# A hybrid mixer block with a gated FFN: staging places, four weight pieces and one product moved around the change of halves

## The chip, the core and the metric

The kernel runs on one core of a Trainium2 chip. The metric is the device time of one execution in microseconds (us), as the median of several runs; less is better. The core has a matrix engine (PE, with its weight loads shown as PEld), a vector engine (DVE), a scalar engine (ACT), a general engine (POOL), and SP, which here does nothing but issue the DMA transfers. Each engine works through its own queue in order, and the queue's order is fixed before the kernel runs.

## The reference

2048 tokens of width 1024 pass one residual block of three mixers with gates, then an FFN with a short convolution, then a norm. The part that the change touches is the second line, the last line, and the end of the first.

```
x = x + merged @ w_o                      # merged: three gated mixers of rms_norm(x)
x = x + conv_ffn(rms_norm(x, norm_ffn_g), ...)
return rms_norm(x, norm_final_g)

def conv_ffn(h, w_in, conv_w, conv_b, w_out):
    u, gv = split(h @ w_in, 2)            # 2816 columns each
    uc = conv_w[0]*u[t-2] + conv_w[1]*u[t-1] + conv_w[2]*u[t] + conv_b
    return (gelu(uc) * gv) @ w_out
```

## The kernel before

Every float32 matrix product is done as three matmuls on operands split into a rounded high part and the remainder. The tokens go through the mixers in four tiles of 512 (the loop at L1031), which write x after the mixers, channels on the partitions, to a buffer x2d in device memory.

The FFN then works on two halves of 1024 tokens. A half has 22 blocks f of 128 FFN columns. in_block (L827) does a block's two input products (u and gv, for two token tiles) with seven block products in place of eight, in the order 1, 2, 6, 5, 3, 7, 4. Each of the seven is twelve matmuls (L837 to L839) of a weight piece against an operand list B[m], and goes into one of four PSUM banks named mm. DVE combines them into u (L868 to L877) and the gate (L880, L881, L883); the convolution is L847 to L849, gelu L850, and gated (L860) writes the result G, split in two, by L861 to L863. At every second block the function mid runs out_group (L913) between product 2 and product 6: it multiplies the G of the two blocks before with w_ffn_out, in 16 tiles of six matmuls (L899 to L901) on banks named ch and mx, and DVE adds each tile to the accumulator acc in SBUF (L903).

Weight pieces live in a ring (ring_tile, L112): six tiles (three wsp, SV, UV, BK), or four while RING[:-2] is set (blocks 2 to 4 of the second half, and the last two blocks of a half). In the first half in_piece (L804) builds a block's seven pieces from four raw weight tiles, 11, 12, 21 and 22 of keepf (L693), with DVE sums at L818 to L821 and a split by ACT and POOL (L823, L824), and stores each to a cache. In the second half it loads the piece from the cache in one transfer of 512 KB. w_out (L886) loads a raw output piece into one of three tiles wraw and splits it (L136, L137).

The operands B of a half are made by ffn_prep (L701), a generator of eight steps. A step loads quarters (128 channels x 512 tokens) of x2d, multiplies each by the norm's factors on DVE (L710), forms differences (minus, L718, DVE) and splits them with ACT and POOL (put, L713 to L715). Steps 1 to 4 load two quarters each, all into wraw; steps 5 to 8 load four each: b11 into the keepf tile 11, b12 into wraw, b22 into 22, b21 into wraw. For the first half, step by step, they go between the products with w_up_rwkv and w_o of the last mixer tile; for the second half, between the tiles of the last two output groups (step, L907). The normalising rows themselves lie in the tiles s1 and 12.

The final norm of the first half is done while the second half begins: after its block 0, finish_sum (L749) squares and sums acc into tiles taken from the ring; after block 1, finish_rstd (L761) and finish_scale (L769) scale acc (ACT, POOL L782, DVE L784) and store it to out, 16 transfers, and load_acc (L962) loads the second half's start values from x2d into the same tiles, 16 more. All DMA is issued by SP from L88, in one queue.

The order of each engine's queue is set by the framework's planner, which takes instructions by priority (the order of the program, raised inside high_priority) as they become ready by its own estimate; the order in the trace therefore differs from the program's at places.

Of the kernel before, what the change touches and what calls it, by code (L numbers as in the profile page):

```python
# [10 lines left out]
F32 = mybir.dt.float32  # L11
# [3 lines left out]
ALU = mybir.AluOpType  # L15
# [4 lines left out]
P = 128  # L20
D = 1024
KB = D // P
TT = 512
# [39 lines left out]
RING = [("wsp", WB)] * WB + [("SV", 1), ("UV", 1), ("BK", 1)]  # L63
# [3 lines left out]
SEVEN = {1: "11", 2: "12", 6: "11", 5: "s1", 3: "12", 7: "21", 4: "22"}  # L67
# [14 lines left out]
def block_kernel(ctx: ExitStack, tc, A, out, T=2048):  # L82
    nc = tc.nc
    NT = T // TT
    te, ve, sc, gp = nc.tensor, nc.vector, nc.scalar, nc.gpsimd
# [18 lines left out]
    sb = ctx.enter_context(tc.tile_pool(name="sb", bufs=1))  # L104
# [17 lines left out]
    ring = {"n": 0, "tags": RING}  # L122

    def ring_tile(dt=F32R):
        tag, bufs = ring["tags"][ring["n"] % len(ring["tags"])]
        ring["n"] += 1
        return sb.tile([P, 2, 512], dt, tag=tag, name="wsp", bufs=bufs)
# [572 lines left out]

    def ffn_prep(hf, B):  # L701

        rsb = [keepf["s1"], keepf["12"]]
        for t in range(2):
            bcast(rsb[t], rs2d[hf * 1024 + t * TT:hf * 1024 + t * TT + TT])

        def quarter(k, t, place=None):
            b = sb.tile([P, 512], F32, tag="wraw", name="wraw", bufs=3) if place is None else keepf[place]
            dma(b, x2d[k, :, hf * 1024 + t * TT:hf * 1024 + t * TT + TT])
            ve.scalar_tensor_tensor(b, b, cc("norm_ffn_g", k), rsb[t], ALU.mult, ALU.mult)  # L710
            return b

        def put(o, src):  # L713
            sc.copy(o[:, 0], src)
            gp.tensor_tensor(o[:, 1], src, o[:, 0].bitcast(F32), ALU.subtract)  # L715

        def minus(dst, a, b):
            ve.tensor_tensor(dst, a, b, ALU.subtract)  # L718

        def blocks(t):  # L720
            return [t[:, :, k, :] for k in range(4)]

        hA = sb.tile([P, 2, 2, 4, TT], F32R, tag="hA", name="hA")
        B[1], B[2] = blocks(hA[:, 0]), blocks(hA[:, 1])
        for k in range(4):
            put(B[1][k], quarter(k, 0))
            put(B[2][k], quarter(4 + k, 0))
            yield
        for m, tag in ((6, "g16"), (5, "z16"), (3, "macc"), (7, "ya")):
            B[m] = blocks(sb.tile([P, 2, 4, TT], F32R, tag=tag, name=f"B{m}"))  # L730
        B[4] = [sb.tile([P, 2, TT], F32R, tag=t, name="B4", bufs=2) for t in ("LP", "LP", "BKt", "BKt")]
        for k in range(4):
            b11, b12, b22, b21 = quarter(k, 0, "11"), quarter(k, 1), quarter(4 + k, 1, "22"), quarter(4 + k, 0)
            minus(b11, b12, b11)
            put(B[5][k], b11)
            minus(b12, b22, b12)
            put(B[3][k], b22)
            minus(b11, b22, b11)
            put(B[6][k], b11)
            put(B[7][k], b12)  # L740
            minus(b21, b11, b21)
            put(B[4][k], b21)
            yield
# [25 lines left out]
    def finish_scale(hf, acc, tk, ssums, o, rs):  # L769
        n = tk.stop - tk.start  # L770
        on_pool = range(1, KB, 2) if n == TT else (1, 3, 5) if tk.stop < 1024 else (1, 3, 5)
        for d in on_pool:
            ac = acc_view(acc, d, tk)
            sc.activation(ac, ac, AF.Identity, scale=cc("norm_final_g", d))
        rp = rows_of(rs, n // P)[:, :n]
        rb = (ring_tile(F32)[:, 0] if o is None else sb.tile([P, TT], F32, tag="LP", name="rb", bufs=2))[:, :n]
        sc.copy(rb, rp)
        for d in range(KB):
            ac = acc_view(acc, d, tk)
            dst = ac if o is None else o[:, d]  # L780
            if d in on_pool:
                gp.tensor_tensor(dst, ac, rb, ALU.mult)  # L782
            else:
                ve.scalar_tensor_tensor(dst, ac, cc("norm_final_g", d), rp if len(ssums) > 2 else rb, ALU.mult, ALU.mult)  # L784
            cols = slice(hf * 1024 + tk.start, hf * 1024 + tk.stop)
            if o is None:
                dma(out[d, :, cols], ac)
            elif d % 2:
                dma(out[d - 1:d + 1, :, cols].rearrange("k p t -> p k t"), o[:, d - 1:d + 1])

    def ffn(prep):
# [8 lines left out]
        acc_tags = [("rq", 1), ("rta", 1), ("rsq", 1), ("rrn", 1), ("rkk", 1), ("rQ", 1), ("rys", 1), ("ry2", 1),  # L800
                    ("bonus", 2), ("bonus", 2), ("sgd", 1), ("rrs", 1), ("rks", 1), ("rvs", 2), ("rvs", 2)]
        B = prep
        for hf in range(T // 1024):
            def in_piece(f, n, m):  # L804

                w = ring_tile()
                hi, lo = w[:, 0], w[:, 1]
                if hf > 0:
                    dma(w.bitcast(F32), cache[7 * f + n])
                    return w  # L810
                if n == 0:
                    for r in ("11", "12", "21", "22"):
                        k0 = 512 * (r[1] == "2")
                        dma(keepf[r], A["w_ffn_in"][f + NF * (r[0] == "2"), :, k0:k0 + 512])
                K = keepf
                with tc.high_priority():
                    if n == 2:
                        ve.tensor_tensor(K["s1"], K["21"], K["22"], ALU.add)  # L818
                        ve.tensor_tensor(K["21"], K["11"], K["21"], ALU.subtract)
                        ve.tensor_tensor(K["11"], K["s1"], K["11"], ALU.subtract)  # L820
                        ve.tensor_tensor(K["12"], K["12"], K["11"], ALU.subtract)  # L821
                    src = K[SEVEN[m]]
                    sc.copy(hi, src)  # L823
                    gp.tensor_tensor(lo, src, hi.bitcast(F32), ALU.subtract)  # L824
                return w

            def in_block(f, G, mid):  # L827
# [40 lines left out]
                ve.tensor_tensor(U0[:, 2:TT + 2], product(2), s1, ALU.add)  # L868
                carry(U0)
                uc0 = conv(U0)  # L870
                if mid is not None:
                    mid()
                ve.tensor_tensor(s1, s1, product(6), ALU.add)
                m5 = product(5)
                U1 = u_tile()
                ve.tensor_tensor(U1[:, 2:TT + 2], m5, s1, ALU.add)
# [102 lines left out]
            for f in range(NF):  # L979
# [17 lines left out]
                if hf > 0 and f == 0:  # L997
                    old_su = []
                    for t in range(2):
                        su = ring_tile(F32)  # L1000
                        old_su.append([su[:, k] for k in range(2)])
                        finish_sum(hf - 1, old, slice(t * TT, t * TT + TT), old_su[t])
                if f == 1:
                    if hf == 0:
                        x2_stats(NT - 1)
                    else:
                        for t in range(2):
                            tk = slice(t * TT, t * TT + TT)
                            rs = finish_rstd(tk, old_su[t])
                            finish_scale(hf - 1, old, tk, old_su[t], None, rs)  # L1010
                    load_acc()
# [282 lines left out]
```

## Time and profile before

| | |
|---|---|
| median of three runs | 3422.11 us (3419.94 to 3427.18) |
| profiled execution | 3428.93 us, span 3427.1 us |
| PE busy | 3172.2 us (93% of the span) |
| DVE busy | 2146.0 us (63%) |
| ACT, POOL busy | 1122.3 us (33%), 986.3 us (29%) |
| DMA | 573.83 MB, mean 167 GB/s |

Times in the rows count from the start of the span. A busy time is that of instructions running, and an idle time is put down to the instruction or transfer whose end came last before the engine went on. Matmuls overlap, so that a matmul's own length (0.39 us) is more than the distance between two of them.

### The profile page before, as it was taken

How to read it: one execution, taken by the hardware profiler on the slowest of the kernel's cores; microseconds unless marked ns; L12 is line 12 of the kernel's file. 1: busy time of each engine (PE TensorE's matmuls, PEld its weight loads, DVE VectorE, ACT ScalarE, POOL GpSimd, SP SyncE). 2: the span in 40 equal slices, each digit the busy share in tenths (PEclk: the TensorE clock that was granted, in tenths of full speed). 3: DMA queues.
4: the chain of work that ended last, by engine and by line, in shares of the span. 5: the costliest groups of instructions: out<-in, count | busy, mean ns of one | idle time of the engine just before them, and what ended most of it. 6: DMA issues, size and time to landing. Idle time of an engine off the chain costs nothing. (4 is left out here: it accounts for less than half of the span.)

```text
span 3427.1 us, 44883 instructions
## 1 busy us (share of the span) xinstructions
PE 3172.2 (93%) x16224; PEld 2489.8 (73%) x16224; DVE 2146.0 (63%) x3950; ACT 1122.3 (33%) x2055; POOL 986.3 (29%) x1128
## 2 busy tenths in 40 slices
PE   6988898999999999999999899999999879999998
PEld 4656676767777677776767677777777668888887
DVE  3987641877436876437874666667667745555556
ACT  3545342433223352223333333233233312121223
POOL 3444443122111221011221644344345511010103
PEclk9999999999999999999999999999999889999999
DMA  7455577345574454653445764444445454443442
GB/s 240 154 178 198 191 236 235 125 126 168 158 228 143 134 167 148 202 186 125 137 153 176 237 226 163 160 169 163 159 169 166 149 188 137 146 141 129 149 146 90
DMA packets 237519, 573.83 MB, mean 167 GB/s; under 512 B 58224, under 2 KB 70128, under 8 KB 237168
## 3 DMA queue, kind: packets, MB, share of 16 engines
q1 hardware_dynamic: 237296, 570.95, 50.7%
q8 instruction: 129, 2.11, 0.3%
q14 instruction: 94, 0.77, 0.1%
HBM read 408.30 MB, written 162.54 MB: 167 GB/s over the span
## 5 line engine op out<-in xcount | busy, mean ns | idle before, releaser
L168 PE MATMUL mm<-h,wsp 128*128 128x512 f32 x4032 | 1101.3, 412 | 10.6 <-ACT h L242 3.0
L168 PEld LDWEIGHTS mm<-h,wsp 128*128 128x128 f32 x4032 | 734.3, 192 | 168.3 <-issue 16.8
L137 POOL TENSOR_TENSOR wsp<-wraw,wsp 128x512 fp32r<-128x512 f32 x204 | 283.8, 1396 | 353.6 <-ACT wsp L136 323.4
L839 PE MATMUL mm<-B,wsp 128*128 128x512 f32 x880 | 347.2, 394 | 1.3 <-POOL wsp L824 1.3
L837 PE MATMUL mm<-B,wsp 128*128 128x512 f32 x880 | 347.6, 395 | 0.0
L838 PE MATMUL mm<-B,wsp 128*128 128x512 f32 x880 | 345.7, 393 | 0.0
L584 DVE TENSOR_TENSOR XX<-XX,As 128x16 f32<-128x16 f32 (+30 forms) x496 | 232.1, 468 | 9.1
L649 POOL TENSOR_SCALAR SV<-SV,dC 64x64 f32<-64x64 f32 x224 | 118.0, 527 | 392.3 <-DVE SV L660 263.0
L168 PE MATMUL mm<-mg,wsp 128*128 128x512 f32 x768 | 195.7, 416 | 33.0 <-DMA wsp<-wc_w_o 17.2
L168 PEld LDWEIGHTS mm<-mg,wsp 128*128 128x128 f32 x768 | 151.9, 201 | 76.8 <-DMA wsp<-wc_w_o 11.4
L847 ACT ACTIVATE tg<-U,cwu 128x512 f32<-128x512 f32 x88 | 71.8, 816 | 391.3 <-DVE U L877 309.5
L839 PEld LDWEIGHTS mm<-B,wsp 128*128 128x128 f32 x880 | 165.7, 188 | 40.5 <-POOL wsp L824 2.2
L838 PEld LDWEIGHTS mm<-B,wsp 128*128 128x128 f32 x880 | 166.0, 189 | 38.1
L837 PEld LDWEIGHTS mm<-B,wsp 128*128 128x128 f32 x880 | 166.2, 189 | 36.4
L136 ACT CAST wsp<-wraw 128x512 fp32r<-128x512 f32 x204 | 125.1, 618 | 172.4 <-PE mm L839 59.4
L837 PE MATMUL mm<-hA,wsp 128*128 128x512 f32 x352 | 140.6, 399 | 30.7 <-DMA wsp<-wc_w_ffn_in 22.3
L858 POOL COPY cwu<-U 128x2 f32<-128x2 f32 x88 | 34.8, 396 | 456.7 <-DVE U L877 294.2
L903 DVE TENSOR_TENSOR acc<-acc,mx 128x512 f32<-128x512 f32 x160 | 109.8, 686 | 87.5 <-PE mx L901 87.0
L586 DVE TENSOR_REDUCE XX<-XX 128x8 f32<-128x16 f32 (+30 forms) x496 | 144.2, 291 | 9.6
L903 DVE TENSOR_TENSOR acc<-acc,ch 128x512 f32<-128x512 f32 x140 | 96.2, 687 | 79.4 <-PE ch L901 78.8
L899 PE MATMUL mx<-G,wsp 128*128 128x512 f32 x320 | 128.5, 402 | 18.6 <-ACT G L862 14.2
L839 PE MATMUL mm<-hA,wsp 128*128 128x512 f32 x352 | 139.3, 396 | 0.0
(375 smaller groups left out, 6055.9 us busy)
## 6 DMA issues: line engine op xcount, KB each, us to landing
wc_w_ffn_in<-wsp SPq DMA_DIRECT2D x154, 512.0 KB, 3.0
wsp<-wc_w_ffn_in SPq DMA_DIRECT2D x154, 512.0 KB, 3.5
wsp<-wc_w_gate SPq DMA_DIRECT2D x144, 512.0 KB, 3.5
wsp<-wc_w_in_mix SPq DMA_DIRECT2D x108, 512.0 KB, 3.4
wc_w_gate<-wsp SPq DMA_DIRECT2D x48, 512.0 KB, 2.9
wsp<-wc_w_o SPq DMA_DIRECT2D x48, 512.0 KB, 4.9
wraw<-in_w_ffn_out SPq DMA_DIRECT2D x88, 256.0 KB, 2.7
wc_w_in_mix<-wsp SPq DMA_DIRECT2D x36, 512.0 KB, 2.9
```

Of the source, the lines that this page charges most:

```text
L136: sc.copy(hi, raw[:, :n])
L137: gp.tensor_tensor(lo, raw[:, :n], hi.bitcast(F32), ALU.subtract)
L168: mm = te.matmul(*args, **kw)
L584: ve.tensor_tensor(xm[:, :, 0:t + 1], X[:, :, 0:t + 1], As[:, 0:t + 1, t].unsqueeze(1).to_broadcast([P, 8, t + 1]), ALU.mult)
L586: ve.tensor_reduce(X[:, :, t:t + 1], xm[:, :, 0:t + 1], AX.X, ALU.add)
L649: gp.tensor_scalar(SV[hs, hh, c + 1, :], SV[hs, hh, c, :], dC[hs, c + 1:c + 2], None, ALU.mult)
L837: te.matmul(acc, w[:, 0, ks], B[m][k][:, 0], start=k == 0, stop=False)
L838: te.matmul(acc, w[:, 0, ks], B[m][k][:, 1], start=False, stop=False)
L839: mm = te.matmul(acc, w[:, 1, ks], B[m][k][:, 0], start=False, stop=k == 3)
L847: sc.activation(uc, U[:, 2:TT + 2], AF.Identity, bias=cw[:, 66 + f:67 + f], scale=cw[:, 44 + f:45 + f])
L899: te.matmul(a, ws[j][0][:, cs], G[j][t][:, 0, tt], start=j == 0, stop=False)
L903: ve.tensor_tensor(ac, ac, a, ALU.add)
```

## The change

Four edits. (1) A quarter of ffn_prep no longer has a place of its own: the quarters go in turn over eight places, three of them wraw, two the tag raw (the tiles of u), and the keepf tiles 22, 11 and 21. (2) The sums of the first half's final norm lie in keepf tiles, not in ring tiles, and its factor rb in wraw. (3) Before that norm's scaling, the first four weight pieces of block 2 (products 1, 2, 6 and 5) are asked for, and the ring is set to four tiles at that point. (4) In every block product 6 is done ahead of mid.

```diff
-        def quarter(k, t, place=None):
-            b = sb.tile([P, 512], F32, tag="wraw", name="wraw", bufs=3) if place is None else keepf[place]
+        staged = [0]
+
+        def quarter(k, t):
+
+            place = ("wraw", "raw", "22", "wraw", "11", "raw", "wraw", "21")[staged[0] % 8]
+            staged[0] += 1
+            if place in keepf:
+                b = keepf[place]
+            else:
+                b = sb.tile([P, TT + 2 * (place == "raw")], F32, tag=place, name="stage", bufs=3 if place == "wraw" else 2)[:, 0:TT]
...
-            b11, b12, b22, b21 = quarter(k, 0, "11"), quarter(k, 1), quarter(4 + k, 1, "22"), quarter(4 + k, 0)
+            b11, b12, b22, b21 = quarter(k, 0), quarter(k, 1), quarter(4 + k, 1), quarter(4 + k, 0)
...
-        rb = (ring_tile(F32)[:, 0] if o is None else sb.tile([P, TT], F32, tag="LP", name="rb", bufs=2))[:, :n]
+        rb = (sb.tile([P, TT], F32, tag="wraw", name="rb", bufs=3) if o is None
+              else sb.tile([P, TT], F32, tag="LP", name="rb", bufs=2))[:, :n]
...
+        ahead = {}
...
             def in_piece(f, n, m):
 
+                if (f, n) in ahead:
+                    return ahead.pop((f, n))
...
+                m6 = product(6)
                 if mid is not None:
                     mid()
-                ve.tensor_tensor(s1, s1, product(6), ALU.add)
+                ve.tensor_tensor(s1, s1, m6, ALU.add)
...
-                        su = ring_tile(F32)
-                        old_su.append([su[:, k] for k in range(2)])
+                        old_su.append([keepf[r] for r in (("22", "11"), ("12", "21"))[t]])
...
+                        ring["tags"] = RING[:-2]
+                        for n, m in list(enumerate(SEVEN))[:4]:
+                            ahead[(2, n)] = in_piece(2, n, m)
```

## Rows read from the trace of the kernel before

**Rows 1.** Busy time by stretch: us, each engine's busy us (instructions), PEclk, DMA, GB/s.

```profile
1868.00:1968.00 100.00, 83.40 (x323) 64.58 (x321) 64.45 (x76) 32.29 (x54) 56.23 (x40) 0.91 0.76 243
1990.00:2590.00 600.00, 580.27 (x2464) 467.35 (x2463) 405.23 (x504) 181.93 (x299) 249.21 (x245) 0.99 0.48 168
2600.00:2704.00 104.00, 83.49 (x325) 63.59 (x324) 82.57 (x102) 32.33 (x54) 60.56 (x46) 0.93 0.51 159
2716.00:2780.00 64.00, 38.65 (x162) 32.32 (x162) 31.86 (x37) 18.29 (x30) 24.04 (x20) 0.73 0.62 209
2780.00:3390.00 610.00, 610.00 (x2649) 497.32 (x2649) 330.19 (x466) 122.96 (x190) 76.68 (x124) 1.00 0.40 134
```

**Rows 2.** Waits of PE, 1990 to 2590: total us, times, longest us.

```profile
PE mx L899 <- ACT G L862: 14.2, 9, 3.1
...
PE mx L900 <- DVE G L863: 2.0, 9, 0.2
```

**Rows 3.** Timeline of PE, start of the first output group: start, length, idle before.

```profile
2013.81 0.50 PE L899 MATMUL mx<-G,wsp 128*128 128x512 f32 x1 [3.10 <-ACT G L862]
```

**Rows 4.** Waits of PE, 1868 to 1968.

```profile
PE mm L168 <- DMA wsp<-wc_w_o: 11.6, 6, 3.5
```

**Rows 5.** Waits of SP's queue, 1868 to 1968.

```profile
SPq L88 <- DVE tw L718: 10.8, 2, 7.0
SPq L88 <- DVE rkk L1215: 6.7, 1, 6.7
```

**Rows 6.** Waits of DVE, 1868 to 1968 (tw holds the tiles 22 and 11).

```profile
DVE tw L710 <- DMA tw<-x2d: 13.8, 4, 5.5
```

**Rows 7.** Timeline of SP: loads of block 0's raw weights (a: tile 12 or 21).

```profile
1810.91 0.43 SPq L88 DMA_DIRECT2D a<-in_w_ffn_in  x1
...
1953.60 0.33 SPq L88 DMA_DIRECT2D tw<-in_w_ffn_in  x1
```

**Rows 8.** Line L715, 1868 to 1968: ns min/median/max, first and last start.

```profile
L715 POOL TENSOR_TENSOR B<-wraw,B x8: 1267/1290/1752, 1902.8 to 1957.6; 128x512 fp32r<-128x512 f32 x8
```

**Rows 9.** Timeline of DVE at 1956.

```profile
1956.61 1.58 DVE L818 TENSOR_TENSOR x<-a,tw 128x512 f32<-128x512 f32 x1 [1.36 <-DMA tw<-in_w_ffn_in]
```

**Rows 10.** Waits of PE, 2590 to 2705.

```profile
PE mm L899 <- DVE acc L903: 9.5, 4, 3.5
PE mx L899 <- DVE acc L903: 4.4, 1, 4.4
```

**Rows 11.** Waits of DVE, 2610 to 2705.

```profile
DVE tw L710 <- DMA tw<-x2d: 9.8, 5, 3.6
...
DVE wraw L710 <- DMA wraw<-x2d: 2.2, 4, 0.8
```

**Rows 12.** Lines L710, L718 and L715, 2610 to 2705: ns min/median/max.

```profile
L710 DVE SCALAR_TENSOR_TENSOR tw<-tw,par,x x4: 747/752/1456, 2616.1 to 2692.1; 128x512 f32<-128x512 f32 x4
...
L718 DVE TENSOR_TENSOR wraw<-tw,wraw x8: 679/682/1181, 2653.9 to 2702.3; 128x512 f32<-128x512 f32 x8
...
L718 DVE TENSOR_TENSOR tw<-tw x4: 1185/1734/1773, 2655.6 to 2700.0; 128x512 f32<-128x512 f32 x4
...
L715 POOL TENSOR_TENSOR B<-wraw,B x8: 1259/1288/1737, 2656.2 to 2704.1; 128x512 fp32r<-128x512 f32 x8
```

**Rows 13.** Timeline of SP around the norm's stores.

```profile
2701.26 4.50 SPq L88 DMA_DIRECT2D wraw<-in_w_ffn_out  x2
...
2738.43 6.12 SPq L88 DMA_DIRECT2D out<-acc  x8
...
2758.82 7.16 SPq L88 DMA_DIRECT2D acc<-x2d  x11
...
2767.90 11.88 SPq L88 DMA_DIRECT2D wsp<-wc_w_ffn_in  x5
```

**Rows 14.** Timeline of PE: end of block 1, and product 2 of block 2.

```profile
2748.10 1.05 PE L219 MATMUL mx<-ident,rs 128*128 128x128 f32 x8
...
2773.97 0.76 PE L837 MATMUL mm<-hA,wsp 128*128 128x512 f32 x1 [22.07 <-DMA wsp<-wc_w_ffn_in]
```

## The prediction

> **What bounds the kernel now.** I read the busy time by stretch first [rows 1], since the page's 93% for PE is an average over very different stages. In the second half's blocks PE is busy in all 610 us: 2649 matmuls, 0.2303 us each. That is the pace of a PE that waits for nothing, and a product of twelve matmuls costs 2.76 us by it. Any stretch can be priced against it, and what is left over is its loss. Blocks of the first half: 2464 x 0.2303 = 567 of 600 us, 33 lost. End of the mixing stage: 323 x 0.2303 = 74 of 100, 26 lost. Change of halves: 75 of 104, 29 lost. Norm of the first half: at most 37 of 64, 27 lost. The edits touch these four stretches and no other, some 115 us together. The reader then asks the waits what ended each loss. In the first half's blocks it is G of the block before [rows 2]; at the end of the mixing stage PE waits for w_o pieces [rows 4] while SP stands behind staging and stores [rows 5] and DVE behind staged operands that haven't landed [rows 6]; at the change of halves PE waits for the accumulations of L903, so for DVE [rows 10], which waits for the same landings [rows 11]; in the norm it is one wait of 22 us for a weight piece [rows 14] queued behind 16 stores and 16 loads [rows 13].
>
> **Output group one product later (M).** In the first half PE does products 1 and 2, then stands until ACT and DVE have written G [rows 3]. The nine groups cost 14.2 + 2.0 us [rows 2]. With product 6 ahead of the group, 2.76 us of work lies where the wait is; the largest wait, 3.10 + 0.2 [rows 3], leaves 0.5. So 16.2 - 0.5 = 15.7; I take 15. The edit adds no instruction. It keeps one of four mm banks through the group, which uses the ch and mx banks, and it needs the third weight piece some 22 us (16 tiles of six matmuls) earlier. Blocks without a group already take product 6 straight behind product 2, and no wait for L824 stands among PE's waits [rows 2], so the piece should be there. If it were late in some blocks, half the gain would go: 8 to 16. In the second half PE has no idle time [rows 1], and M is worth nothing there.
>
> **Eight places, end of the mixing stage (B).** Today a second-loop step uses 11 and 22 for every k, so its load waits until the step before has finished with them: SP stood 10.8 us on L718 [rows 5], and DVE 13.8 us on landings in those two tiles [rows 6]. Both queues are in order, so the w_o pieces behind come late, 11.6 us for PE [rows 4], and PE restarts cold after some. With eight places a load can run two steps ahead. SP's wait for the store of rkk, 6.7 us [rows 5], is itself DVE standing late. If all of the 11.6 went: +12, +16 with cold restarts. Against it: place 21 is new in the rotation, as its last quarter. Before, block 0's raw weight 21 was loaded at 1810.9 [rows 7], long ahead; now it can go only when the last put ends, 1957.6 + 1.3 = 1958.9 [rows 8], and takes about 3 us, the interval from the load of a raw weight at 1953.6 [rows 7] to L818, which waited for it [rows 9]. So L818, at 1956.6, would come at about 1962, 5 us later, if the staging ended no earlier; PE's third product hangs on it. Ends: -5 and +16. I take +4: half the wait less part of the late weight.
>
> **Eight places, change of halves (A).** PE's waits there are 9.5 + 4.4 us for L903 [rows 10]; smaller waits and matmuls at a lower clock (0.93 in the mean [rows 1]) make up the rest of the 29. DVE's waits on landings are 9.8 + 2.2 us [rows 11]. More places should take most of those. What comes next is DVE and POOL themselves. L718 in place takes 1.73 us beside POOL's subtraction, 0.68 in most of the others; L710 takes 0.75 to 1.46 [rows 12]. Suppose the two never overlap. Then 24 x 0.75 (L710) + 16 x 0.68 (L718) + 32 x 1.26 (L715, and the eight output pieces of L137 taken alike) = 69 us, and some 10 us of gating and weight splits of block 21 on the same tiles make 79, in a stretch of 2616 to 2705, 89 us. So at most 10 us can go. I take 6; ends 0 and 10.
> The Trainium skill ("SBUF — State Buffer", section "SBUF: two separate sides") says that a DVE operation with two SBUF inputs and a GpSimd operation that reads SBUF take the shared port pair as an exclusive lock, one fully blocking the other. The trace agrees with it by the 1.73 against 0.68. It speaks against this part: earlier landings only bring the two engines to the same lock sooner, and the cap is 10 us where the waits alone would promise 12.
>
> **Sums, rb and four pieces ahead of the stores (N).** The sums move from two ring tiles to idle raw-weight tiles, and rb to wraw. The instructions are the same. Ring tiles are no longer held by the sums. The four loads ask for ring tiles freed by products 2, 7, 4 and 6 of block 1. PE can then run products 1, 2, 6 and 5 of block 2 while stores and loads flow; today only product 1. But product 3 of block 2 still waits behind the same 32 transfers. If it starts when product 2 starts today, 2773.97 [rows 14], three products are gained, 8.3 us, and the cold restart of twelve matmuls stays. Against it: SP is in order, and the fourth load may wait for the last product of block 1, which ends at 2748 today [rows 14], where the first store went at 2738.4 [rows 13]: up to 9.7 us later. The window has room for that: 11 loads took 7.16 us [rows 13], 0.65 each, so 32 need 20.8 us, while 2738.4 to 2767.9 is 29.5. So the delay ends between 0 and 9.7. Above: the planner that orders the queues may put the later pieces ahead of the stores too; the whole hole plus the cold restart (twelve matmuls at 1.2 instead of 2.4 GHz, the clock's mean in the stretch being 0.73 [rows 1]: 12 x 0.23 = 2.8) is 25. Ends -1 and +25; I take 8.
>
> **Sum.** 15 + 4 + 6 + 8 = 33 us. The profiled execution took 3428.93 us (span 3427.1 and 1.8 around it), 6.8 above the median 3422.11: 3396 by its own time, 3389 by the median.
>
> **Rivals.**
> 1. Only M pays. Staging stays bound by the DVE-POOL chain, and block 0's late weight eats B; the norm's hole moves whole to product 3 with SP held back. For it: the 79 of 89 us, and 9.7 against 8.3. Against: waits on landings in both stretches. Gain 15 + 0 to 5: 3402 to 3407.
> 2. The hole closes. The planner also puts products 3, 7 and 4 ahead of the stores. For it: two output pieces of the group at block 3 were loaded at 2701.26 [rows 13], ahead of block 1's pieces. Against: before, pieces 2 to 4 of block 2 had free tiles by 2748 and still went behind all 32 transfers. N is 25 instead of 8: 3372.
> 3. It doesn't do what it says: the planner had its own order, and the new one only reshuffles. M alone speaks against it, since PE's order there was the program's. Within 0.2%: 3415 to 3429.
> 4. Slower. DVE is in order, and a staged operand blocks it until it lands. The 48 quarters cost 13.8 + 9.8 + 2.2 = 25.8 us now [rows 6, 11], 0.5 each. With more places the planner starts loads and multiplies sooner, among block 21's gating and the mixing chain, each as close behind its load as it thinks safe. If the mean wait rises to 2 us, 48 x 2 - 25.8 = 70 us more stand on DVE. About 60 of it would reach PE where DVE is the late engine: 3422 - 33 + 60 = 3449. It decides from about 1.2 us each (48 x 1.2 - 25.8 = 32). Against it: a larger buffer count gives each load a longer lead.
>
> **How the numbers follow.** Forecast (gain 20 to 45): 0.56. Rival 1: 0.17. Rival 2: 0.11. Rival 3: 0.08. Rival 4: 0.08. Faster by over 0.2% (about what a measurement of this kernel can tell from no change, 6.8 us) is the first three, 0.84; same 0.08; slower 0.08. The ends of the four terms add to 2 and 67 us; all at one end is unlikely, and 11 to 56 leaves out rivals 3 and 4 and the far end of 2: 3366 to 3411.
>
> **What would show it.** M: waits of L899 for L862 in the first half's blocks under 2 us, product 6 ahead of L899. B: waits for w_o under 6 us, and whether L818 of block 0 waits for weight 21. A: DVE's waits for x2d small, L718 and L710 as slow as now. N: four products of block 2 ahead of the hole, the next load still behind the loads of acc, the hole ending near 2773.97 less the gains before it. I am wrong if PE stands behind L824 ahead of the groups, if the first store slips by over 10 us, or if DVE's waits for x2d grow.

## The result, and the profile after

The changed kernel takes 3378.48 us in the median, the kernel before 3421.03 in the same comparison: a ratio of 0.9871, with a 95% interval of 0.9845 to 0.9898. Run once more beside other kernels it came to 0.9876 (0.9857 to 0.9896). One of the four executions behind the median of 3378.48 ran at a granted clock of 0.556 and took 5019.63 us; the ratio leaves it out, and the median of the other three is 3375.32. By the two ratios 42 to 44 us are gone; 33 were forecast, and the range held. The four terms behind the 33 came out quite differently from each other, though, and the rest of the document is about them.

The profiled execution of the changed kernel took 3373.29 us (span 3371.4), that of the kernel before 3428.93. The spans differ by 55.7 us, more than the ratio says: the executions of before lay between 3408 and 3431 us over all comparisons, so its profiled one is among the longer ones. Line numbers shift: before's L710, L718, L715 are now L718, L726, L723; the products are L849 to L851 (before L837 to L839), the output group L912 to L914 (L899 to L901), the accumulation L916 (L903), block 0's sums L830 (L818).

First the busy time by stretch, of the changed kernel. The columns are those of [rows 1], and the four stretches answer to its first four rows.

```profile
1891.00:1947.00 56.00, 48.69 (x193) 37.72 (x194) 37.56 (x39) 18.02 (x30) 37.77 (x27) 0.94 0.76 251
1992.00:2540.00 548.00, 547.16 (x2378) 447.46 (x2378) 377.26 (x492) 180.24 (x292) 264.00 (x238) 1.00 0.50 176
2554.00:2658.00 104.00, 85.11 (x330) 64.61 (x328) 88.69 (x102) 36.61 (x61) 68.99 (x49) 0.90 0.49 149
2679.00:2740.00 61.00, 41.93 (x179) 34.19 (x178) 30.76 (x38) 14.32 (x23) 22.29 (x20) 0.78 0.65 227
```

Priced as in the prediction, the first half's blocks have nothing left to lose: 2378 x 0.2303 = 547.7 of 548 us. The change of halves still loses 104 - 330 x 0.2303 = 28 us, as much as before (29). To compare kernels whose stretches start at different times, the table below measures each stage on PE from the start of one product to the start of another. It is worked out from the traces, and every later section goes by it.

```
profiled execution   w_o's last   block 0   block 2   block 20    2nd half    its block 1   rest
(us)                 product set  to 2      to 20     to 2nd      block 0     to block 4
                     to block 0                       half        to block 1* (norm)
before                 66.6        43.9      580.5     112.0        28.1        109.8       592.5
changed                55.6        44.9      547.9     110.9        28.2        103.0       589.7
changed, again         56.1        46.4      548.0     113.0        27.9        105.8       590.6
e1_group_only          69.4        43.9      550.3     109.1        28.0        110.0       590.4
e2_stage_only          57.5        44.8      576.8     116.3        28.1        111.1       592.4
e3_norm_only           68.7        43.8      576.7     109.9        28.5        102.1       590.2
e4_acc_later           56.2        44.8      546.9     111.2        28.4        100.0       588.8
e5_fill_wait           68.6        43.4      576.5     110.7        29.3        109.3       592.3
e6_put_on_act          54.7        44.8      547.4      95.1        28.4        104.6       589.3
e7_old_second          56.3        44.8      548.8     107.5        28.2        102.1       589.8
e8_both                56.5        44.8      546.2     108.2        28.7        101.6       589.3
e10_rows_psum_eight    55.9        44.8      547.3     100.8        35.0        101.8       589.8
e11_rows_psum_old      56.9        44.8      547.3      98.0        35.1        104.5       589.4
* to the fourth product of block 1
```

Ahead of these stages the executions differ too: the first column begins between 1881.4 and 1896.3 us after the span's start, in kernels that hardly differ up to there. A stage is therefore a finer measure than a whole time. From before to changed the columns give -11.0, +1.0, -32.6, -1.1, +0.1, -6.8 and -2.8, and the start of the first -2.5. The kernel before's own row is long in one place: e2 and e3 have its code in blocks 2 to 20 and take 576.8 and 576.7 there, so some 4 of the 32.6 us belong to the execution and not to the edit.

**First half's blocks.** PE's waits from 1935 to 2545 (us in total, times, the longest). The two rows of [rows 2] are gone. What is left are waits for weight splits (L835 and L836, before L823 and L824), all but 0.8 us of them before 1992, so in blocks 0 and 1. They are no work of the change: the kernel before has them at the same place, 2.8 and 1.3 us between 1950 and 2004, all of it ahead of the window of [rows 2].

```profile
PE mm L849 <- ACT wsp L835: 3.2, 1, 3.2
PE mm L851 <- POOL wsp L836: 2.8, 5, 1.0
PE mm L168 <- DMA wsp<-wc_w_o: 0.5, 1, 0.5
```

**End of the mixing stage.** PE's waits from 1860 to 1960, against the 11.6 us of [rows 4]:

```profile
PE mm L168 <- DMA wsp<-wc_w_o: 6.1, 4, 3.2
```

and DVE's in the same stretch, against the 13.8 of [rows 6] and 2.9 more in wraw, which those rows don't show:

```profile
DVE stage L718 <- DMA stage<-x2d: 6.0, 2, 3.1
DVE x L830 <- DMA a<-in_w_ffn_in: 4.6, 1, 4.6
DVE tw L718 <- DMA tw<-x2d: 4.5, 1, 4.5
```

The first and third rows are the staged operands, 10.5 us together. The second is block 0's raw weight 21, late because its tile was a staging place, with its 4.6 us in place of the 1.36 in [rows 9]. Its instruction, L830, starts 2.1 us after block 0's first product, where L818 had started 3.7 us ahead of it; but PE stands only 1.0 us in block 0's third product, which needs it (0.7 before).

**Change of halves.** DVE's waits from 2560 to 2662, against the 12.0 us of [rows 11]:

```profile
DVE a L718 <- DMA a<-x2d: 0.9, 1, 0.9
DVE tw L718 <- DMA tw<-x2d: 0.4, 1, 0.4
DVE stage L718 <- DMA stage<-x2d: 0.4, 1, 0.4
```

PE's from 2545 to 2655, against [rows 10]:

```profile
PE mm L912 <- DVE acc L916: 9.3, 5, 2.9
PE mx L912 <- DVE acc L916: 5.3, 1, 5.3
PE ch L912 <- DVE acc L916: 2.3, 1, 2.3
```

So the landings no longer hold DVE, and DVE holds PE a little longer than before: 16.9 us, where [rows 10] and 1.1 us on ch made 15.0. What changed are the lengths of instructions (lines of DVE and POOL, 2560 to 2662: ns min/median/max, first and last start):

```profile
L718 DVE SCALAR_TENSOR_TENSOR stage<-stage,par,x x9: 740/1172/1751, 2580.7 to 2627.0; 128x512 f32<-128x512 f32 x9
...
L726 DVE TENSOR_TENSOR stage<-tw,stage x4: 682/1449/1761, 2603.6 to 2631.2; 128x512 f32<-128x512 f32 x4
...
L137 POOL TENSOR_TENSOR wsp<-wraw,wsp x8: 1581/1732/1783, 2575.1 to 2618.0; 128x512 fp32r<-128x512 f32 x8
```

The kernel before, same operation on POOL, 2610 to 2705:

```profile
L137 POOL TENSOR_TENSOR wsp<-wraw,wsp x8: 1271/1302/1755, 2622.0 to 2666.1; 128x512 fp32r<-128x512 f32 x8
```

These are groups by tile, and their medians (0.75 and 0.68 us in [rows 12], 1.17 and 1.45 here) make the change look larger than the sums do. Added up from the traces, the 24 multiplies take 24.8 us, before 25.5; the 16 differences 18.1, before 15.6; POOL's 28 subtractions of put 44.8, before 41.6; its eight splits of output pieces 13.8, before 11.7. Over all 24 multiplies the median went from 0.75 to 0.96 us. The other profiled kernels that stage as before have 21.1 to 23.6 us of multiplies and 16.1 to 16.7 of differences, so against them both are longer, by some 2 us each. Another thing moved: 12 of the 16 differences and 24 of the 28 subtractions started inside the stage before, and all of them do now.

**Norm of the first half.** SP's timeline (start, length, count), as in [rows 13]:

```profile
2699.93 12.76 SPq L88 DMA_DIRECT2D out<-acc  x15
2713.13 0.33 SPq L88 DMA_DIRECT2D out<-x  x1
2713.52 9.79 SPq L88 DMA_DIRECT2D acc<-x2d  x15
2723.66 0.32 SPq L88 DMA_DIRECT2D x<-x2d  x1
2724.38 2.36 SPq L88 DMA_DIRECT2D wsp<-wc_w_ffn_in  x4
```

and the hole on PE, ahead of product 3 of block 2, against [rows 14]:

```profile
2730.47 0.76 PE L849 MATMUL mm<-B,wsp 128*128 128x512 f32 x1 [16.82 <-DMA wsp<-wc_w_ffn_in]
```

Four products run before the hole; it is 16.8 us instead of 22.1, and the next load still stands behind all 32 transfers.

### The profile page after: what moved, and what is told of

Read it like the earlier page. It is cut to its first block, busy times and chain, and to the rows that moved or that the text cites. A ratio compares the mean times of both kernels' runs of the same rounds, so it can differ in the third digit from the quotient of the medians.

```text
span 3371.4 us, 44873 instructions
## 1 busy us (share of the span) xinstructions
PE 3156.2 (94%) x16224; PEld 2483.5 (74%) x16224; DVE 2135.6 (63%) x3950; ACT 1126.0 (33%) x2055; POOL 1018.8 (30%) x1128
## 5 line engine op out<-in xcount | busy, mean ns | idle before, releaser
L137 POOL TENSOR_TENSOR wsp<-wraw,wsp 128x512 fp32r<-128x512 f32 x204 | 286.7, 1410 | 363.0 <-ACT wsp L136 305.6
L849 PE MATMUL mm<-B,wsp 128*128 128x512 f32 x880 | 348.2, 396 | 16.8 <-DMA wsp<-wc_w_ffn_in 16.8
L851 PE MATMUL mm<-B,wsp 128*128 128x512 f32 x880 | 347.2, 395 | 1.8 <-POOL wsp L836 1.8
L849 PEld LDWEIGHTS mm<-B,wsp 128*128 128x128 f32 x880 | 165.8, 188 | 53.9 <-issue 17.2
L851 PEld LDWEIGHTS mm<-B,wsp 128*128 128x128 f32 x880 | 165.5, 188 | 42.0 <-POOL wsp L836 3.1
L916 DVE TENSOR_TENSOR acc<-acc,mx 128x512 f32<-128x512 f32 x160 | 109.8, 686 | 85.5 <-PE mx L914 85.2
L916 DVE TENSOR_TENSOR acc<-acc,ch 128x512 f32<-128x512 f32 x140 | 96.1, 686 | 81.0 <-PE ch L914 81.0
L849 PE MATMUL mm<-hA,wsp 128*128 128x512 f32 x352 | 140.3, 399 | 3.5 <-ACT wsp L835 3.2
L851 PE MATMUL mm<-hA,wsp 128*128 128x512 f32 x352 | 140.4, 399 | 1.0 <-POOL wsp L836 1.0
L850 PE MATMUL mm<-hA,wsp 128*128 128x512 f32 x352 | 139.9, 398 | 0.0
```

The costliest lines, as they stand in the source:

```text
L137: gp.tensor_tensor(lo, raw[:, :n], hi.bitcast(F32), ALU.subtract)
L849: te.matmul(acc, w[:, 0, ks], B[m][k][:, 0], start=k == 0, stop=False)
L850: te.matmul(acc, w[:, 0, ks], B[m][k][:, 1], start=False, stop=False)
L851: mm = te.matmul(acc, w[:, 1, ks], B[m][k][:, 0], start=False, stop=k == 3)
L916: ve.tensor_tensor(ac, ac, a, ALU.add)
```

## The experiments

Each ratio is the time over that of the kernel before in the same comparison, with its 95% interval.

**The parts alone.** Three kernels, each the kernel before with some of the four edits.

e1_group_only:

```diff
+                m6 = product(6)
                 if mid is not None:
                     mid()
-                ve.tensor_tensor(s1, s1, product(6), ALU.add)
+                ve.tensor_tensor(s1, s1, m6, ALU.add)
```

> The kernel before with the fourth edit alone: product 6 is done ahead of mid. Theory: the whole loss of the first half's blocks against a PE that waits for nothing (33 us by matmul count) goes, because the short wait for G also lowers PE's clock for the matmuls behind it and both go together; 25 to 33 us faster than the kernel before. Rival, the sum of the prediction: only the idle time goes, 15 us faster, and the rest of what the two profiles show in that stretch belongs to the other edits or to the run of before that was profiled.

Measured: 0.9912 (0.9893 to 0.9932), 30 us less, and 30 less in the stage of blocks 2 to 20 (580.5 to 550.3). Of PE's waits, 2000 to 2551, this is left:

```profile
PE mx L900 <- DVE acc L904: 1.4, 1, 1.4
PE mm L839 <- POOL wsp L824: 1.0, 1, 1.0
```

The edit alone is worth 30 us by the whole time (23 to 37 by the interval), and 26 in this stage against e2 and e3, which have the stage without it (576.8 and 576.7). Its two rows of waits were 16.2.

e2_stage_only:

```diff
-        def quarter(k, t, place=None):
+        def quarter(k, t):
+            place = ("wraw", "raw", "22", "wraw", "11", "raw", "wraw", "21")[staged[0] % 8]
```

> The kernel before with the first edit alone: the quarters go over eight places. Theory: some 10 us faster, all of it at the end of the mixing stage (waits for w_o halved), and nothing at the change of halves, although DVE's waits for landings there fall from 12 us to under 3: DVE's multiplies and differences and POOL's subtractions and splits get longer instead. Rival, as predicted: 4 us in the one place and 6 in the other, with the lengths of those operations unchanged.

Measured: 0.9986 (0.9972 to 0.9999), 4.8 us less, where 10 were expected. The first stage is 9 us shorter than before's (66.6 to 57.5) and 11 to 12 shorter than in e1, e3 and e5 (68.6 to 69.4), which stage as before does. The next one is 0.9 longer, and the change of halves is 4 longer than before's. PE's waits from 1890 to 1948 answer to [rows 4]:

```profile
PE mm L168 <- DMA wsp<-wc_w_o: 5.0, 4, 2.7
```

One half of the edit gains, and the other seems to give part of it back; two executions of one kernel differ by 2 us in that stage (e9 below).

e3_norm_only:

```diff
-        rb = (ring_tile(F32)[:, 0] if o is None else ...
+        rb = (sb.tile([P, TT], F32, tag="wraw", name="rb", bufs=3) if o is None
...
+                        ring["tags"] = RING[:-2]
+                        for n, m in list(enumerate(SEVEN))[:4]:
+                            ahead[(2, n)] = in_piece(2, n, m)
```

> The kernel before with the second and third edits: sums and rb out of the ring, four weight pieces of block 2 asked for ahead of the norm's stores. Theory: 7 to 8 us faster; four products of block 2 run before the hole, which shrinks from 22 to about 17 us and now stands ahead of product 3 (fifth in order). Rival: the stores slip behind the pieces and nothing is gained, 0 to 2 us.

Measured: 0.9987 (0.9972 to 1.0002). The norm's stage is 7.7 us shorter (109.8 to 102.1); of the whole time 4.5 us, with zero at the edge of the interval. The hole on PE, the longest wait of its timeline there:

```profile
2759.46 0.77 PE L841 MATMUL mm<-B,wsp 128*128 128x512 f32 x1 [18.03 <-DMA wsp<-wc_w_ffn_in]
```

The three add up to 39 us, against 42 to 44 for all together.

**Why the group's edit is worth more than its waits.** e5_fill_wait is the kernel before with eight matmuls into a PSUM bank that nobody reads, ahead of each of the first half's groups: 9 x 8 x 0.23 = 16.6 us of useless work where PE idled 16.2.

```diff
+                last_w = []
...
+                    last_w[:] = [w, B[m]]
...
+                if mid is not None and hf == 0:
+                    idle = mm_bank()
+                    w, b = last_w
+                    for k in range(8):
+                        ks = slice(k % 4 * P, (k % 4 + 1) * P)
+                        te.matmul(idle, w[:, 0, ks], b[k % 4][:, 0], start=k == 0, stop=k == 7)
                 if mid is not None:
```

> The kernel before, with eight more matmuls (on product 2's operands, into a bank nobody reads, 8 x 0.23 = 1.8 us) between product 2 and the output group, in the first half alone: work that does nothing, laid into the wait for G. Theory: half of what product 6 gave (the 30 us of the fourth edit alone) is not the wait but PE's lower clock behind it; a PE that is busy while G comes keeps its clock, so this kernel is 8 to 15 us faster than the kernel before although it does 9 x 1.8 = 17 us more work. Rival: only the idle time counts; the added work takes its place, and where the wait was shorter it adds to the time: 0 to 5 us slower.

Measured: 1.0003 (0.9988 to 1.0019). Busy time of the first half's blocks, and two of PE's waits from 2008 to 2585:

```profile
2008.00:2585.00 577.00, 570.11 (x2452) 458.60 (x2453) 394.28 (x489) 175.88 (x289) 241.72 (x238) 1.00 0.48 167
```

```profile
PE mm L839 <- ACT tg L852: 3.1, 6, 0.7
PE mx L907 <- ACT G L864: 1.7, 1, 1.7
```

The granted clock rose from 0.99 to 1.00, and yet the time stayed, so the theory that the clock behind each wait is half of the gain falls. The clock's own share can be read. Behind five of the nine waits (these five are 1.4 to 3.1 us long) the kernel before has stretches at half the clock, 1.2 GHz, in which matmuls start 0.43 us apart; the first of them, and the granted clock in it:

```profile
2015.00:2018.00 3.00, 3.00 (x9) 2.33 (x8) 1.38 (x2) 2.13 (x4) 3.00 (x3) 0.50 0.35 93
```

With the fill there is no such stretch between 1963 and 2635. What the gain is made of was then read from the distances between starts of matmuls, wherever one is over 0.26 us, less the 0.23 of a running product (worked out from the traces):

```
1990 to 2590 (changed: to 2540)                 before   with the fill   changed
at the group's first matmul (L899, 9 times)       15.7        2.4          -
at its second (L900, 9 times)                      4.5        0.5          -
at product 2 (L837, 7 times)                       4.6        4.1          -
matmuls in the stretches at half the clock         7.8        0           1.2
the rest                                           1.6        7.2         1.8
sum                                               34.2       14.2         3.0
```

The row of product 2 is in the waits of the kernel before too, 1990 to 2590, and [rows 2] leaves it out:

```profile
PE mm L837 <- ACT tg L850: 3.5, 7, 0.6
```

The fill took 20 us off the excess and cost 16.6 itself, so it had 3 us to give, less than the comparison tells apart. It removed all 7.8 us of the half clock; but matmuls of the group that start 0.3 to 0.5 us apart at the full clock came in (most of its 7.2), which is not explained here. Product 6 in the same place costs nothing, since it had to be done anyway, and the excess goes from 34.2 to 3.0. Useful work in the hole is what counted. In e2 and e3, whose stage is 4 us shorter than before's, the same excess is 32.0 and 30.8, with 6.8 and 6.4 in it for the half clock.

**The norm's remaining hole.** e4_acc_later is the changed kernel with the 16 loads of acc after block 2 instead of after block 1.

```diff
                             finish_scale(hf - 1, old, tk, old_su[t], None, rs)
+                if f == (1 if hf == 0 else 2):
                     load_acc()
```

> The changed kernel, with the second half's 16 loads of acc asked for after block 2 instead of after block 1. Theory: the hole ahead of product 3 is time that its weight stands in SP's queue behind 16 stores and these 16 loads (0.65 us each, 10 us); with the loads behind the weights it starts about 10 us sooner, and acc is wanted only in block 3, so 8 to 10 us faster than the changed kernel. Rival: the stores alone, which wait for the norm's scaling, set the end of the hole, or the loads come too late for the output group of block 3; within 2 us of the changed kernel, or slower.

Measured: 0.9863 (0.9839 to 0.9888), against the changed kernel's 0.9871 and 0.9876: no difference. The norm's stage is 3 to 6 us shorter (100.0 against 103.0 and 105.8). SP's timeline:

```profile
2708.02 1.39 SPq L88 DMA_DIRECT2D wsp<-wc_w_ffn_in  x3
2709.46 12.14 SPq L88 DMA_DIRECT2D acc<-x2d  x15
...
2722.93 1.66 SPq L88 DMA_DIRECT2D wsp<-wc_w_ffn_in  x3
```

and PE's, at the weight pieces:

```profile
2713.54 0.76 PE L849 MATMUL mm<-B,wsp 128*128 128x512 f32 x1 [5.60 <-DMA wsp<-wc_w_ffn_in]
...
2729.02 0.77 PE L849 MATMUL mm<-hA,wsp 128*128 128x512 f32 x1 [5.16 <-DMA wsp<-wc_w_ffn_in]
```

The hole of 16.8 became 5.6 and 5.2. SP's queue is in order: the loads of acc hold up pieces wherever they stand, only other pieces now. The 8 to 10 us that were expected of it did not come.

**What holds the change of halves.** The theory after the first results: DVE and POOL lengthen each other's instructions, as [rows 12] suggested, and the waits for landings were only what hid it. The rival: DVE waits for the loads in another form, and fewer or other places would mend it.

e6_put_on_act leaves POOL's subtraction out of the second half's put and has ACT write a second copy in its place, so the second half's remainders are not computed:

```diff
             sc.copy(o[:, 0], src)
-            gp.tensor_tensor(o[:, 1], src, o[:, 0].bitcast(F32), ALU.subtract)
+            if hf == 0:
+                gp.tensor_tensor(o[:, 1], src, o[:, 0].bitcast(F32), ALU.subtract)
+            else:
+                sc.copy(o[:, 1], src)
```

> The changed kernel, with the remainder of the second half's operands written by an ACT copy (which leaves out the subtraction, so that the second half's remainders are wrong) instead of POOL's subtraction. Theory: at the change of halves the gain of the staging went to DVE and POOL, which lengthen each other; without 24 of POOL's operations there DVE's multiplies and differences take 0.75 and 0.68 us again (1.2 and 1.4 now), and PE's loss of 28 us in that stretch falls by 10 or more. Rival: the order of DVE's queue is what holds PE (staging ahead of the accumulations); then the lengths fall, but the loss stays within 5 us of what it is.

Measured: 0.9808 (0.9788 to 0.9828), and the change of halves in 95.1 us, 16 less than in the changed kernel. Lines, 2560 to 2662:

```profile
L718 DVE SCALAR_TENSOR_TENSOR stage<-stage,par,x x9: 736/739/753, 2583.8 to 2622.3; 128x512 f32<-128x512 f32 x9
...
L137 POOL TENSOR_TENSOR wsp<-wraw,wsp x8: 1276/1296/1732, 2577.7 to 2614.3; 128x512 fp32r<-128x512 f32 x8
```

With POOL's subtractions gone, most of DVE's multiplies take 0.74 us (all 24 together 19.2 us, 24.8 in the changed kernel), the 16 differences 11.5 (18.1), and POOL's other work is back at 1.30. DVE's order in the stage is that of the changed kernel but for one pair, so the order alone is not what holds it. But e6 takes two things away at once, the lengthening and the 44.8 us in which POOL itself works on the operands (28 operations, not the 24 of the expectation); their shares in the 16 us are not told apart by it.

e7_old_second is the changed kernel with the eight places in the first half's staging only:

```diff
+            if hf > 0:
+                place = "wraw" if staged[0] < 8 else ("11", "wraw", "22", "wraw")[staged[0] % 4]
             staged[0] += 1
```

> The changed kernel, with the eight places for the first half's operands alone; the second half's use wraw, 11 and 22 as before. Theory: the eight places earn their 12 us at the end of the mixing stage and lose 2 to 4 at the change of halves (block 20's first product to the second half's first: 111, 116, 111 us with them, 112, 109, 110 without), so this kernel is 0 to 4 us faster than the changed one, and that stretch takes about 110 us. Rival: the staging helps in both places, and this kernel is 5 us or more slower.

Measured: 0.9839 (0.982 to 0.9857), 3365.08 us, the lowest ratio of the kernels that compute all of the block. The change of halves takes 107.5 us, 3.4 less than in the changed kernel (5.5 less than in its second execution), although DVE's waits for landings are back (2550 to 2650):

```profile
DVE tw L720 <- DMA tw<-x2d: 9.4, 5, 3.5
...
DVE stage L720 <- DMA stage<-x2d: 1.8, 4, 1.0
```

So the rival falls, and in the second half the eight places cost a little; in e7 the multiplies take 21.8 us and the differences 16.1 (24.8 and 18.1 in the changed kernel). The stage accounts for 3 to 5 us; the rest of the 12 us between 0.9839 and 0.9876 is not placed, and the two were not timed in one comparison. e8_both is e7 with e4's edit too.

> The changed kernel with the eight places for the first half's operands alone and the loads of acc behind block 2. Theory: the two add, 47 + 0 to 4 us faster than the kernel before, so 3368 to 3372 where that takes 3419. Rival: the later loads of acc only help behind the new staging; 42 us or less.

Measured: 0.9842 (0.9822 to 0.9862), not to be told from e7; e4's edit adds nothing here either. Its change of halves takes 108.2 us, short like e7's. e9_changed_again is the changed kernel without an edit, for the spread of its stages.

> The changed kernel itself, beside the next two on one chip. Theory and rival alike: 42 to 44 us faster than the kernel before; a stretch from block 20 to the second half of 109 to 113 us, and 55 to 57 us from the first product with w_o to the first block.

Measured: 0.9876 (0.9857 to 0.9896). Its change of halves took 113.0, so two executions of one kernel differ by 2 us there.

e10_rows_psum_eight asks whether the lengthening needs both inputs of DVE in SBUF: the changed kernel, with the norm's rows for the second half's multiplies copied into two PSUM banks.

```diff
+        if hf > 0:
+            rsp = [mm_bank() for t in range(2)]
+            for t in range(2):
+                sc.copy(rsp[t], rsb[t])
...
-            ve.scalar_tensor_tensor(b, b, cc("norm_ffn_g", k), rsb[t], ALU.mult, ALU.mult)
+            ve.scalar_tensor_tensor(b, b, cc("norm_ffn_g", k), rsp[t], ALU.mult, ALU.mult)
...
-                        out_tile(G, ws[d // 4], d, tk, "mm")
+                        out_tile(G, ws[d // 4], d, tk, "mm" if final else "ch")
```

> The changed kernel, with the second half's norm rows copied once into two of the mm banks of PSUM, from which the staged multiply reads them (the output tiles of the last group then go to the ch and mx banks). Nothing is left out. Theory: it is two SBUF inputs that make DVE and POOL lengthen each other; with one input in PSUM the 24 multiplies take 0.75 us each whatever POOL does (1.0 to 1.2 now), and POOL's subtractions and splits lengthen less, so the change of halves is 5 to 12 us shorter (99 to 106 for 111), the whole 5 to 12 us faster than the changed kernel. Rival: the lengthening comes from POOL's traffic whatever DVE reads; the multiplies stay above 1 us and the time is the changed kernel's, or worse since two banks are gone.

Measured: 0.9859 (0.9839 to 0.9878). Lines of DVE, 2540 to 2660:

```profile
L724 DVE SCALAR_TENSOR_TENSOR stage<-stage,par,mm x15: 731/733/748, 2576.8 to 2630.6; 128x512 f32<-128x512 f32 x15
L724 DVE SCALAR_TENSOR_TENSOR tw<-tw,par,mm x6: 732/733/736, 2583.5 to 2629.3; 128x512 f32<-128x512 f32 x6
...
L732 DVE TENSOR_TENSOR stage<-tw,stage x4: 677/1448/1767, 2598.7 to 2625.9; 128x512 f32<-128x512 f32 x4
```

None of the 24 multiplies is over 0.748 us, with POOL at work all the while, and the differences (L732), still with two inputs from SBUF, are as long as in the changed kernel (18.1 us together in both). The Trainium skill ("SBUF — State Buffer", section "SBUF: two separate sides") says just this, a lock between a GpSimd operation that reads SBUF and a DVE operation with two SBUF inputs; the run agrees by 0.73 against up to 1.77 us. The change of halves is 10 us shorter (100.8), but the next stage is 7 longer (35.0): with two of the four mm banks taken, the last output tiles run on ch and mx, and the trace has them between the products of block 0: 18 matmuls, 4.1 us of the 7, are only moved from one stage to the other. The two stages together take 135.7 us, against 139.1 in the changed kernel and 135.6 in e7. So 7 us less of multiplies on DVE (17.6 for 24.8) were worth 3.4 us in these stages, and by the whole time (0.9859 against 0.9876 beside it) nothing that the comparison tells apart; 5 to 12 had been expected. DVE's order in the stage differs from the changed kernel's here, as it does in e7, so the 3.4 are not the lengthening's alone.

e11_rows_psum_old is the same edit on e7.

> The same rows in PSUM with the eight places for the first half's operands alone (wraw, 11 and 22 for the second half's). Theory: staging in eight places costs at the change of halves because it packs DVE's and POOL's work closer; with the multiplies out of that, either staging gives the same within 3 us there, and this kernel is the fastest or equal to the one with eight places. Rival: landings then hold DVE back again (12 us in the kernel before), and this one is 5 us or more slower than with eight places.

Measured: 0.9874 (0.9853 to 0.9895); the two stages take 133.1 us, the least of any kernel that does POOL's subtraction, but the whole is no faster than e7. What the stages win, the whole time doesn't show.

## Why the prediction was right, and where its terms were off

**The total** was right in sign and within the range (42 to 44 us against 33). Two terms were about half of what came, one had the wrong sign, and one was near. That the sum came so close is in part luck: the edit of M alone gave 26 to 30 us, and what M and B gave above their terms covered what A did not give.

**M, output group one product later: 15 predicted, 26 to 30 measured.** The mechanism was right: product 6 lies where the wait was, and both rows of [rows 2] are gone. The step that failed is the size, "the nine groups cost 14.2 + 2.0 us". The same text had priced the stretch at 33 us lost [rows 1], and took only two of the three waits in it. The rest was the wait at product 2 (4.6 us, 3.5 in the view), matmuls at half the clock behind the waits (7.8), 4 us by which the distance between starts exceeds the waits of the view (15.7 + 4.5 against 16.2), and 1.6 us of smaller distances. With no other loss in that stretch, the 33 was the better estimate. That the fourth bank, held through the group, or the earlier weight piece would hurt was rightly held unlikely: in e1 the wait for L824 is 1.0 us.

**B, end of the mixing stage: 4 predicted, about 9 measured.** The stage is 11 us shorter than before's (13 to 14 shorter than that of e1, e3 and e5), and the next one 1 longer. About 1 us more comes off: in every kernel with the eight places PE waits 2.1 to 3.8 us just ahead of this stage (3.2 in the changed one), where the others wait at most 0.5. Counted from the first product with w_up_rwkv to block 0, the time is 81.3 us against 90.5 (80.9 to 82.4 with the eight places, 90.5 to 93.1 without). "Half the wait less part of the late weight" was off at both terms. Waits for w_o fell by half as said (11.6 to 6.1). Within the stage they fell further, from 11.4 to 2.9 us, since 3.2 of the 6.1 lie ahead of it; and what matmuls lose in stretches at half the clock fell from 5.0 to 2.5 us. The two make up the 11. The late weight came as foreseen, DVE standing 4.6 us at L830, and the stage behind it is 1 us longer, not 5: that PE's third product hangs on it in full was supposed, not read, and PE stood 1.0 us there.

**A, change of halves: 6 predicted, +1 to -5 measured.** The waits went as predicted, 12.0 to 1.7 us, and nothing came of it. The step that failed is "more places should take most of those" being read as time, under a cap worked out by "suppose the two never overlap". That sum also counts 32 operations of POOL where the trace has 36 (28 of L715 and the eight of L137): it makes 74 us, not 69, and the cap 5 us, not 10. And it prices them at the shortest lengths in [rows 12]. With operands at hand sooner, DVE's busy time in the stretch grows from 82.57 of 104 us [rows 1] to 88.69 of 104, POOL's from 60.56 to 68.99, and PE waits for L916 no less than before. e6 shows that 16 us go when POOL's subtraction does; how much of that is the lengthening and how much POOL's own work stays open, and e10, which undoes the lengthening of the multiplies, gives 3.4 us with an order of DVE that differs too. The sentence on the lock spoke against this part, and should have moved the term to zero.

**N, sums, rb and four pieces: 8 predicted, 4 to 8 measured in the stage** (109.8 to 103.0 and 105.8; 102.1 in e3), though the whole time of e3 shows only 4.5, with zero at the edge. Four products ahead of the hole, the next load behind the loads of acc: as said. The first store went at 2699.9, 7.6 us late once the 46.1 us gained ahead of it are taken off, inside the 0 to 9.7 allowed. The slack of 8.7 us in that window swallowed most of it: product 3 starts 2.6 us after the place of product 2 in [rows 14], so 5.7 of the 8.3 are left; the other 1 us was not traced to a cause.

**Rivals.** 1 (only M pays) falls with B and N, by their stages; M itself was worth more than the rival's whole gain. 2 (the hole closes) did not occur; e4 shows that the hole moves rather than closes. 3 falls with the 42 to 44 us. 4 (staged multiplies block DVE) found its opposite: DVE waits less on landings in both stretches. (Its 25.8 us of such waits before leave out the 2.9 on wraw at the end of the mixing stage.)

**The better version** is e7, the change without eight places in the second half: 3365.08 us, 0.9839. It beats the kernel before clearly. Against the changed kernel its interval just touches that of the second comparison (0.9857) and overlaps that of the first (0.9845 to 0.9898), and the two were not timed side by side; that it is faster than the changed kernel is likely, with e8 at 0.9842 beside it, but not shown.

## What to carry to other kernels

Price a stretch by its count of matmuls times the undisturbed pace before adding up its waits; where one edit removes the only cause of loss there, expect most of that difference, and take the rows of idle time as the lower end. Before a landing wait on DVE is shortened, look at the lengths of DVE's and POOL's operations beside each other: here they already lengthened each other, and earlier operands bought nothing. Add up a whole group of instructions before reading a change out of the median of a part of it. A staging scheme that pays in one stage needn't be used in the other.

## What the runs showed of the hardware that was not expected

With one input in PSUM, 24 DVE multiplies of 128x512 kept to 0.731 to 0.748 us beside a busy POOL; the same 24 with both inputs in SBUF took 0.74 to 1.77 us, with a median of 0.96 (e10, changed). Of nine waits of PE, of 1.0 to 3.1 us, five were followed by matmuls at half the clock, 0.43 us apart, which lost 7.8 us in all (before). Filling these waits with useless matmuls removed every such stretch (e5); 20 us of waits and slower matmuls went, 16.6 us of useless ones came, and the time stayed (e5: 1.0003).
